# Weight parts in whole tiles, and tokens weighted before they are split, in a two-layer decoder kernel with experts

## The chip, the core and the metric

The kernel runs on one core of one Trainium2 chip. The metric is device time in microseconds (us), 1342.04 as the median of three runs (1341.5 to 1342.77) before the change.

## The reference, cut to what matters

256 tokens of width 1024 pass two layers; each adds a mixer, a cross attention and a feed-forward part to `x`. In the second layer the last part is a choice of 2 of 8 experts for each token:

```python
h = rmsnorm(x, norm_ffn_w[l])          # x * rsqrt(mean(x*x) + EPS) * w
logits = h @ router_w                  # 8 experts
top_v, top_i = top_k(logits, 2)        # gates: softmax of the two
for e in range(8):                     # width 2816
    y = y + gates[..., e:e+1] * ((silu(h @ w_gate[e]) * (h @ w_up[e])) @ w_down[e])
x = x + y
```

Everything is fp32. A product of two fp32 matrices is made of rounded parts: each operand is written as a high part (rounded) and a low part (the rest), and three products (low with high, high with low, high with high) are added.

## The kernel before

**Weights.** All weights come in tiles of 128x2048 fp32 (1 MB) in one fixed order (`weight_order`). SP loads them into staging tiles (`wst`, `wsp`), as many ahead as staging tiles are free (`stage`, `load` L173). Each tile is split: ACT copies it, rounded, into the high part `wh`, in two halves of 1024 columns; DVE subtracts, staged minus high, into the low part `wl`. In the layers `halve` (L185) does that, in 512 or 1024 columns; in the expert stage `high` (L236) and `low` (L247) do it, each for half a tile. The parts live in tiles of half a weight (`Halves` L89): five buffers each of `wh` and `wl` in the layers, seven and six in the expert stage (`HALVES` L37, L376).

**The expert stage** has its order written out by hand for PE, ACT and DVE (L1559). 264 weight tiles are used one after the other, each in one call of `slot` (L261). In the slot of tile t ACT rounds tile t+2, DVE subtracts tile t+1, and PE uses tile t. An expert is 11 chunks of three tiles: two of gate and up weights, one of down weights. Four experts are *long* (up to 128 tokens, three products a part, 12 matmuls of 512 columns a tile), four are *short* (up to 64 tokens; high and low part side by side in one operand, 8 matmuls a tile). Long and short chunks alternate after six long ones, and the last are short; the down tile of a chunk is used one chunk of its kind later.

Small steps are *posted* to a later slot and a place in it: before the first high half on ACT (`act`), between the two halves on ACT or DVE (`act mid`, `dve mid`), or in or behind PE's products (`pe mid`, `pe`). They are: the silu, the multiplication and the split of the hidden values (`chain`, L1373 and L1411), turned by PE in between (tile `et`); the marks that list an expert's tokens as one-hot columns (`mark` L1506, tile `oh`); the gather of an expert's tokens; and, when an expert is left (`leave` L1437), the transposes of its marks (`eo`), the split of its result (`yh`, `yl`), the scatter (`ez`) and the addition to `x`.

**The gather** (L1224) makes an expert's tokens out of `x` and the one-hot columns: `x` is split into `hmh` and `hml` (`halves` L1210, ACT then DVE), for each of 8 slices of the width PE adds four products into PSUM, so that the two parts come out summed; ACT multiplies by the norm's weight, rounded (`highs` L1244), DVE multiplies again and subtracts (`lows` L1248). The first gather runs before the expert stage, behind routing, among the steps of `columns` (the norm's factor `ncol`); the others are posted, one slice a slot. Routing itself (`route` L1103) follows the last addition to `x` in the cross attention.

`slot` and `low`, which the change reorders, in the words of the code:

```python
        self.places("act")
        self.high(t + 2, 0)
        self.low(t + 1, 0)
        self.places("dve mid", "act mid")
        self.high(t + 2, 1)
        self.low(t + 1, 1)
        w = self.ready.pop(key)
        products[0](*w)
        self.places("pe mid")
        products[1](*w)
        self.places("pe")
```

Of the kernel before, what the change touches and what calls it, by code (L numbers as in the profile page):

```python
# [7 lines left out]
F32 = mybir.dt.float32  # L8
# [28 lines left out]
HALVES = (5, {"wh": 2, "wl": 1})  # L37
# [49 lines left out]


class Halves:  # L89


    def __init__(self, *tiles):
        self.tiles = tiles

    def __getitem__(self, at):
        p, s = at
        h = s.start // 1024
        return self.tiles[h][p, s.start - h * 1024:s.stop - h * 1024]


class Trunk:
# [80 lines left out]
    def halves(self, name):  # L182
        return Halves(*[next(self.pools[name]).tile([P, 1024], F32R, name=name) for _ in range(2)])

    def halve(self, slot, st):  # L185

        nc, tc = self.nc, self.tc
        wh, wl = self.halves("wh"), self.halves("wl")
# [47 lines left out]
    def high(self, i, q):  # L236

        if i >= len(self.order) or i < self.nsplit:
            return
        if q == 0:  # L240
            self.stage()
            self.parts[i] = *self.loaded.pop(0), self.halves("wh"), self.halves("wl")
        _, st, wh, _ = self.parts[i]
        s = slice(q * 1024, (q + 1) * 1024)
        self.nc.scalar.activation(wh[:, s], st[:, s], AF.Copy)  # L245

    def low(self, i, q):  # L247
        if i not in self.parts:
            return
        slot, st, wh, wl = self.parts[i]  # L250
        s = slice(q * 1024, (q + 1) * 1024)
        with self.tc.issue_after(self.hold.ins) if self.hold else nullcontext():
            self.nc.vector.tensor_tensor(wl[:, s], st[:, s], wh[:, s].bitcast(F32), op=ALU.subtract)  # L253
        if q == 1:
            self.hold = None
            self.ready[self.order[i][0]] = wh, wl
            del self.parts[i]
            self.free.append(slot)
            self.stage()

    def slot(self, key, *products):  # L261
        t = self.nused
        assert self.order[t][0] == key, (self.order[t][0], key)
        self.now += 1
        if t + 1 < len(self.order) and t + 1 >= self.nsplit and t + 1 not in self.parts:
            self.high(t + 1, 0)
# [12 lines left out]
        self.nused += 1  # L279

    def rest(self):

        self.now += 1
        self.places("act", "dve mid", "act mid", "pe mid", "pe")


    def build(self):
# [6 lines left out]
        self.wp = pool("wp", HALVES[0])  # L294
        self.pools = {n: repeat(self.wp) for n in ("wh", "wl")}
# [77 lines left out]
        with tc.tile_pool(name="emid", bufs=1) as self.md, tc.tile_pool(name="ewkb", bufs=2) as self.wb, \  # L373
                tc.tile_pool(name="wst2", bufs=STAGES[1]) as wst2, ExitStack() as more:
            self.free += [slot(wst2)] * STAGES[1]
            for n, k in HALVES[1].items():  # L376
                p = more.enter_context(tc.tile_pool(name=f"{n}2", bufs=k))
                self.pools[n] = cycle([p] * k + [self.wp] * HALVES[0])
# [630 lines left out]
    def xattn(self, l):  # L1009
# [191 lines left out]
    def moe(self, j, l):  # L1201
# [22 lines left out]
        def gather(lists, xg):  # L1224
# [12 lines left out]
            def products(k):  # L1237
                ps[k] = self.psum(name="xg")
                for s in range(2):
                    for i in range(NT):  # L1240
                        nc.tensor.matmul(ps[k][:, lo:lo + w], hm[1 - s][:, i, k * P:(k + 1) * P], ohs[:, i, lo:lo + w],
                                         start=s == 0 and i == 0, stop=s == 1 and i == NT - 1)

            def highs(k):  # L1244
                for t, c in zip(xg, at):
                    self.split_hi(t[:, k, 0], ps[k][:, c], norm.w[:, k:k + 1])

            def lows(k):  # L1248
                for t, c in zip(xg, at):
                    self.gathered = self.split_lo(t[:, k, 0], t[:, k, 1], ps[k][:, c], norm.w[:, k:k + 1])  # L1250
# [11 lines left out]
            def steps():  # L1262
                for k in range(KD):
                    products(k)
                    highs(k)
                    lows(k)
# [4 lines left out]
            def spread(n):  # L1271

                for k in range(KD):
                    self.post(n + k, "pe", lambda k=k: products(k))
                    self.post(n + k + 1, "act mid", lambda k=k: highs(k))
                    self.post(n + k + 2, "dve mid", lambda k=k: lows(k))
                self.post(n + KD, "pe", scales)
                self.post(n + KD + 1, "dve mid", keep_scales)
# [88 lines left out]
        def long(x, xr):  # L1367
# [5 lines left out]
            def chain(pg):  # L1373
# [10 lines left out]
                self.post(1, "dve mid", lambda: nc.vector.scalar_tensor_tensor(  # L1384
# [3 lines left out]
                self.post(2, "dve mid", lambda: self.split_lo(*h, pt))  # L1388
# [8 lines left out]
        def short(x, xr):  # L1397
# [13 lines left out]
            def chain(pg):  # L1411
# [13 lines left out]
                self.post(2, "dve mid", lambda: nc.vector.tensor_tensor(s, s, pt[:, 2:4, :], op=ALU.mult))  # L1425
                self.post(2, "act mid", lambda: self.split_hi(hs[:, :, 0, :], s))
                self.post(3, "dve mid", lambda: self.split_lo(hs[:, :, 0, :], hs[:, :, 1, :], s))
# [9 lines left out]
        def leave(ps, oh, gate):  # L1437
# [18 lines left out]
            for n in range(2):  # L1456
                self.post(1 + n, "act", lambda n=n: self.split_hi(y[n][0], ps[n]))
                self.post(1 + n, "dve mid", lambda n=n: self.split_lo(*y[n], ps[n]))
            self.post(1, "dve mid", lambda: nc.vector.tensor_copy(oT, po[:, 0:T]))
            for n in range(2):  # L1460
                for i in range(NT):
                    pz = self.psum(name="ez")
                    self.post(2 + 2 * n + i, "pe", lambda pz=pz, i=i, n=n: scatter(pz, i, n))
                    self.post(3 + 2 * n + i, "dve mid", lambda pz=pz, i=i, n=n: add(pz, i, n))
# [51 lines left out]
        def prepare():  # L1516
# [3 lines left out]
            halves(1, 1)  # L1520
            return at, steps()

        def spread(n):
            marks, _, rest = lists_of(n)
            for i, m in enumerate(marks):
                self.post(1 + i, "dve mid", m)
# [84 lines left out]
    def final_weights(self):  # L1611
# [11 lines left out]
        for k in range(8):  # L1623
            b = k // 4
            self.post(1 + k, "dve mid", lambda k=k: diagonal(k))
# [26 lines left out]
def pack(inputs):  # L1652
# [23 lines left out]
    def chan(m):  # L1676

        L = m.shape[0]
        if m.ndim == 2:
# [17 lines left out]
                              [bias, chan(np.stack([g["norm_final_w"]] * DEPTH))], axis=2)  # L1697
    a["xq"] = fm(g["xattn_w_q"])
# [24 lines left out]
```

## Time and profile before

| what | value |
|---|---|
| median of three runs | 1342.04 us (1341.5 to 1342.77) |
| the profiled execution, its own time | 1343.5 us |
| its span, first to last instruction | 1341.6 us |
| mean granted TensorE clock | 0.990 |
| ACT, busy | 937.6 us (70%) |
| POOL, busy | 7.5 us (1%) |
| DMA, over the span | 368.06 MB, mean 274 GB/s |

The profile is that of one execution. Engines: PE multiplies, PEld loads PE's stationary operand, DVE is the vector engine, ACT the scalar engine, POOL GpSimd, SP the queue that issues loads. A row of a timeline gives the start in us from the span's start, the length, the engine, the line, the operation, output and inputs, shapes and, in brackets, how long the engine sat idle before it and what ended that. `x4` behind a row means four like it, one after the other. Matmuls are pipelined: the distance of two starts is what one costs.

### The profile page before, as it was taken

To read this page: it belongs to the slowest core of one execution; us is meant where nothing else is said; L and a number is where in the kernel's file an instruction comes from. 1 tells how busy PE (TensorE), PEld (TensorE's weight loads), DVE (VectorE), ACT (ScalarE), POOL (GpSimd) and SP (SyncE) were. 2 spreads that over 40 slices of the span, in tenths; PEclk is the share of its full clock that TensorE was granted. 3 is DMA by queue.
4 is the path that set the end of the run, shared out by engine and by line. 5 is a ranking of instruction groups with operands and counts; after the bars stand their busy time and mean duration, and the time that the engine had idled before them with its cause. 6 is when DMAs were issued, how large, how long until landed. Compare 5 with 4: busy or idle time off the path is not lost.

```text
span 1341.6 us, 20691 instructions
## 1 busy us (share of the span) xinstructions
PE 1293.9 (96%) x7301; PEld 1087.7 (81%) x7301; DVE 1162.9 (87%) x2057; ACT 937.6 (70%) x1502; POOL 7.5 (1%) x30
## 2 busy tenths in 40 slices
PE   9999999999999999989999999999999999999995
PEld 8978989999999878778877787777877778777773
DVE  8998877666677988579999999999999999999997
ACT  7565575444465556558788788887888887887884
POOL 0000000000000000000000000000000000000000
PEclk9999999999999999979999999999999999999998
DMA  8423625555544424549999999999999999999990
GB/s 326 158 96 118 228 95 194 187 187 189 187 165 151 164 95 160 194 149 338 343 405 386 338 371 413 379 402 338 355 412 384 394 380 337 404 407 371 392 351 34
DMA packets 67567, 368.06 MB, mean 274 GB/s; under 512 B 5744, under 2 KB 6000, under 8 KB 38016
## 3 DMA queue, kind: packets, MB, share of 16 engines
q1 hardware_dynamic: 67136, 365.59, 72.1%
q8 instruction: 59, 0.97, 0.3%
q0 software_dynamic: 320, 1.08, 0.2%
q14 instruction: 52, 0.43, 0.1%
HBM read 365.60 MB, written 1.05 MB: 273 GB/s over the span
## 4 chain that ended last, share of the span: by engine, by line
PE 68%; DVE 20%; issue 7%; ACT 5%; DMA 0%; DVEq 0%; SPq 0%; ACTq 0%
DVE wl L253 12%; PE fm L437 5%; PE fm L439 5%; PE fm L438 5%; PE eg L437 5%; PE eg L439 5%; PE eg L438 5%; PE ed L1433 4%; PE ed L437 2%; PE ed L438 2%; PE ed L439 2%; PE et L1420 2%; PE pr L437 2%; PE pr L438 2%; PE pr L439 2%
## 5 line engine op out<-in xcount | busy, mean ns | idle before, releaser
L253 DVE TENSOR_TENSOR wl<-wst,wh 128x1024 fp32r<-128x1024 f32 x294 | 348.9, 1222 | 0.0
L245 ACT ACTIVATE wh<-wst 128x1024 fp32r<-128x1024 f32 x294 | 295.6, 1053 | 0.0
L195 DVE TENSOR_TENSOR wl<-wst,wh 128x512 fp32r<-128x512 f32 x328 | 214.8, 688 | 87.9 <-ACT wh L191 87.7
L253 DVE TENSOR_TENSOR wl<-wsp,wh 128x1024 fp32r<-128x1024 f32 x232 | 276.1, 1222 | 1.5 <-PE eg L438 1.5
L191 ACT ACTIVATE wh<-wst 128x1024 fp32r<-128x1024 f32 x164 | 171.3, 1062 | 143.7 <-PE fm L439 88.5
L245 ACT ACTIVATE wh<-wsp 128x1024 fp32r<-128x1024 f32 x232 | 234.4, 1054 | 0.3 <-PE eg L439 0.3
L437 PE MATMUL fm<-hTh,wl 128*128 128x256 f32 x736 | 207.6, 282 | 1.0 <-DVE wl L195 1.0
L438 PE MATMUL fm<-hTl,wh 128*128 128x256 f32 x736 | 206.2, 280 | 0.0
L439 PE MATMUL fm<-hTh,wh 128*128 128x256 f32 x736 | 205.9, 280 | 0.0
L1409 PE MATMUL eg<-wl,xs 128*128 128x512 f32 x352 | 143.9, 409 | 5.9 <-DVE wl L253 5.9
L437 PE MATMUL eg<-wh,xg 128*128 128x512 f32 x352 | 141.2, 401 | 0.0
L437 PEld LDWEIGHTS fm<-hTh,wl 128*128 128x128 f32 x736 | 138.3, 188 | 1.9 <-DVE wl L195 1.2
L438 PE MATMUL eg<-wl,xg 128*128 128x512 f32 x352 | 139.8, 397 | 0.0
L439 PE MATMUL eg<-wh,xg 128*128 128x512 f32 x352 | 139.8, 397 | 0.0
L438 PEld LDWEIGHTS fm<-hTl,wh 128*128 128x128 f32 x736 | 138.2, 188 | 0.8 <-issue 0.2
L439 PEld LDWEIGHTS fm<-hTh,wh 128*128 128x128 f32 x736 | 138.7, 188 | 0.0
L1409 PE MATMUL eg<-wh,xs 128*128 128x512 f32 x352 | 138.6, 394 | 0.0
L1433 PE MATMUL ed<-wl,ehh 128*128 128x512 f32 x176 | 78.1, 444 | 13.5 <-DVE wl L253 12.2
L1409 PEld LDWEIGHTS eg<-wl,xs 128*128 128x128 f32 x352 | 66.3, 188 | 23.4 <-DVE wl L253 10.7
L439 PEld LDWEIGHTS eg<-wh,xg 128*128 128x128 f32 x352 | 66.8, 190 | 15.7
L437 PEld LDWEIGHTS eg<-wh,xg 128*128 128x128 f32 x352 | 67.0, 190 | 14.8
L438 PEld LDWEIGHTS eg<-wl,xg 128*128 128x128 f32 x352 | 66.9, 190 | 14.8
(339 smaller groups left out, 2257.0 us busy)
## 6 DMA issues: line engine op xcount, KB each, us to landing
wst<-in_moe_gu_dram SPq DMA_DIRECT2D x115, 1024.0 KB, 7.0
wsp<-in_moe_gu_dram SPq DMA_DIRECT2D x61, 1024.0 KB, 6.9
wsp<-in_moe_w_down_dram SPq DMA_DIRECT2D x55, 1024.0 KB, 7.2
wst<-in_moe_w_down_dram SPq DMA_DIRECT2D x33, 1024.0 KB, 7.3
wst<-in_ffn_gu_dram SPq DMA_DIRECT2D x22, 1024.0 KB, 4.9
wst<-in_w_in_fm_dram SPq DMA_DIRECT2D x16, 1024.0 KB, 4.9
wst<-in_ffn_w_down_dram SPq DMA_DIRECT2D x11, 1024.0 KB, 4.9
wst<-in_w_in_tm_dram SPq DMA_DIRECT2D x8, 1024.0 KB, 5.0
```

Source lines behind the costliest of these rows:

```text
L191: self.halved = nc.scalar.activation(wh[:, s], st[:, s], AF.Copy)
L195: nc.vector.tensor_tensor(wl[:, s], st[:, s], wh[:, s].bitcast(F32), op=ALU.subtract)
L245: self.nc.scalar.activation(wh[:, s], st[:, s], AF.Copy)
L253: self.nc.vector.tensor_tensor(wl[:, s], st[:, s], wh[:, s].bitcast(F32), op=ALU.subtract)
L437: nc.tensor.matmul(out, ll, rh, start=start, stop=False)
L438: nc.tensor.matmul(out, lh, rl, start=False, stop=False)
L439: nc.tensor.matmul(out, lh, rh, start=False, stop=stop)
L1409: nc.tensor.matmul(pg, both[:, c], w[:, fs], start=c == 0 and w is wl, stop=c == KD - 1 and w is wh)
L1420: nc.tensor.matmul(pt[:, b, :], g[:, b * P:(b + 1) * P], comb, start=True, stop=True)
L1433: nc.tensor.matmul(ps[n], h[:, k], w[:, fs], start=start and w is wl, stop=stop and w is wh)
```

## The change

Weight parts become whole tiles of 128x2048, three buffers each of `wh` and `wl` for the whole kernel. ACT still rounds in two halves; in the expert stage DVE subtracts a whole tile at once, and the steps of `dve mid` come behind it, in a place now called `dve`. `halve` in the layers keeps its pieces. In the short chunk the rounding of the hidden values goes from `act mid` of one slot to `act` of the next.

Tokens are multiplied by the norm's weight before they are split, by POOL (`xw`, four products of 128x512), with the weight as a row on all partitions, loaded by a broadcast from a new input `wrow` into the tile that later holds the output. That tile is also a staging tile; it is withheld until the last product is issued. The gather keeps the two parts apart, side by side in PSUM, and ACT copies both with one instruction; DVE's `lows` are gone.

```diff
-HALVES = (5, {"wh": 2, "wl": 1})
+SPLITS = {"wh": 3, "wl": 3}
...
+    def parts_of(self):
+        return [self.wp.tile([P, 2048], F32R, name=n, bufs=SPLITS[n]) for n in ("wh", "wl")]
...
-    def low(self, i, q):
+    def low(self, i):
         if i not in self.parts:
             return
-        slot, st, wh, wl = self.parts[i]
-        s = slice(q * 1024, (q + 1) * 1024)
+        slot, st, wh, wl = self.parts.pop(i)
         with self.tc.issue_after(self.hold.ins) if self.hold else nullcontext():
-            self.nc.vector.tensor_tensor(wl[:, s], st[:, s], wh[:, s].bitcast(F32), op=ALU.subtract)
-        if q == 1:
-            self.hold = None
-            self.ready[self.order[i][0]] = wh, wl
-            del self.parts[i]
-            self.free.append(slot)
-            self.stage()
+            self.nc.vector.tensor_tensor(wl, st, wh.bitcast(F32), op=ALU.subtract)
+        self.hold = None
+        self.ready[self.order[i][0]] = wh, wl
+        self.free.append(slot)
+        self.stage()
...
         self.places("act")
         self.high(t + 2, 0)
-        self.low(t + 1, 0)
-        self.places("dve mid", "act mid")
+        self.low(t + 1)
+        self.places("dve", "act mid")
         self.high(t + 2, 1)
-        self.low(t + 1, 1)
...
             self.o = self.spare()().rearrange("p (i d) -> p i d", i=NT)
+            self.later = self.free.pop()
+            self.wrow = self.o[:, 0, :]
+            nc.gpsimd.dma_start(self.wrow, a["wrow"].to_broadcast([P, D]))
             self.spare()
...
         def halves(i, n):
             s = slice(n * 512, (n + 1) * 512)
-            self.split(hm[0][:, i, s], hm[1][:, i, s], self.x[:, i, s])
+            xw = wb.tile([P, 512], F32, name="xw", tag="yh" if n else "yl")
+            nc.gpsimd.tensor_tensor(xw, self.x[:, i, s], self.wrow[:, s], op=ALU.mult)
+            self.split(hm[0][:, i, s], hm[1][:, i, s], xw)
...
             def products(k):
-                ps[k] = self.psum(name="xg")
+                ps[k] = self.psum((P, 2, 2 * P), "xg")
                 for s in range(2):
                     for i in range(NT):
-                        nc.tensor.matmul(ps[k][:, lo:lo + w], hm[1 - s][:, i, k * P:(k + 1) * P], ohs[:, i, lo:lo + w],
-                                         start=s == 0 and i == 0, stop=s == 1 and i == NT - 1)
-
-            def highs(k):
-                for t, c in zip(xg, at):
-                    self.split_hi(t[:, k, 0], ps[k][:, c], norm.w[:, k:k + 1])
-
-            def lows(k):
-                for t, c in zip(xg, at):
-                    self.gathered = self.split_lo(t[:, k, 0], t[:, k, 1], ps[k][:, c], norm.w[:, k:k + 1])
+                        nc.tensor.matmul(ps[k][:, s, lo:lo + w], hm[s][:, i, k * P:(k + 1) * P], ohs[:, i, lo:lo + w],
+                                         start=i == 0, stop=i == NT - 1)
+
+            def keep(k):
+                for t, c in zip(xg, at):
+                    self.gathered = nc.scalar.activation(t[:, k], ps[k][:, :, c], AF.Copy)
...
-                    self.post(n + k + 1, "act mid", lambda k=k: highs(k))
-                    self.post(n + k + 2, "dve mid", lambda k=k: lows(k))
+                    self.post(n + k + 1, "act mid", lambda k=k: keep(k))
...
-                self.post(2, "act mid", lambda: self.split_hi(hs[:, :, 0, :], s))
-                self.post(3, "dve mid", lambda: self.split_lo(hs[:, :, 0, :], hs[:, :, 1, :], s))
+                self.post(3, "act", lambda: self.split_hi(hs[:, :, 0, :], s))
+                self.post(3, "dve", lambda: self.split_lo(hs[:, :, 0, :], hs[:, :, 1, :], s))
...
             halves(1, 1)
+            self.free.append(self.later)
             return at, steps()
```

## Rows read from the trace of the kernel before

**Rows 1.** The page, engines: busy us, share of the span, instructions.
```profile
PE 1293.9 (96%) x7301; PEld 1087.7 (81%) x7301; DVE 1162.9 (87%) x2057; ACT 937.6 (70%) x1502; POOL 7.5 (1%) x30
```

**Rows 2.** The page, costliest groups: count, busy us, mean ns of one, idle before.
```profile
L253 DVE TENSOR_TENSOR wl<-wst,wh 128x1024 fp32r<-128x1024 f32 x294 | 348.9, 1222 | 0.0
...
L195 DVE TENSOR_TENSOR wl<-wst,wh 128x512 fp32r<-128x512 f32 x328 | 214.8, 688 | 87.9 <-ACT wh L191 87.7
...
L437 PE MATMUL fm<-hTh,wl 128*128 128x256 f32 x736 | 207.6, 282 | 1.0 <-DVE wl L195 1.0
```

**Rows 3.** Timeline of PE: first such pair's hole, one pair, last hole.
```profile
674.35 0.50 PE L1433 MATMUL ed<-wl,ehh 128*128 128x512 f32 x1 [0.15 <-DVE wl L253]
...
700.72 0.48 PE L1409 MATMUL eg<-wl,xs 128*128 128x512 f32 x1
...
704.47 0.40 PE L1433 MATMUL ed<-wl,ehh 128*128 128x512 f32 x1
...
705.30 0.50 PE L1433 MATMUL ed<-wl,ehh 128*128 128x512 f32 x1 [0.20 <-DVE wl L253]
...
705.87 1.00 PE L1420 MATMUL et<-comb,eg 128*128 128x64 f32 x8
...
716.22 0.48 PE L1409 MATMUL eg<-wl,xs 128*128 128x512 f32 x1
...
1203.21 0.50 PE L1433 MATMUL ed<-wl,ehh 128*128 128x512 f32 x1 [0.19 <-DVE wl L253]
```

**Rows 4.** Timeline of ACT in that pair.
```profile
698.38 2.00 ACT L245 ACTIVATE wh<-wst 128x1024 fp32r<-128x1024 f32 x2
701.00 0.38 ACT L447 ACTIVATE ehh<-et 128x256 fp32r<-128x256 f32 x1 [0.62 <-PE et L1381]
701.28 3.90 ACT L245 ACTIVATE wh<-wsp 128x1024 fp32r<-128x1024 f32 x4
```

**Rows 5.** Timeline of DVE in that pair.
```profile
701.41 0.43 DVE L451 TENSOR_TENSOR ehl<-et,ehh 128x256 fp32r<-128x256 f32 x1
...
702.89 4.63 DVE L253 TENSOR_TENSOR wl<-wsp,wh 128x1024 fp32r<-128x1024 f32 x4
```

**Rows 6.** Timeline of DVE where a long expert is left.
```profile
732.15 0.29 DVE L1509 TENSOR_SCALAR oh<-twice,sorted 128x128 fp32r<-128x128 bf16 x1 [2.24 <-PE eo L1445]
...
734.62 0.42 DVE L451 TENSOR_TENSOR ehl<-et,ehh 128x256 fp32r<-128x256 f32 x1
...
736.08 2.35 DVE L253 TENSOR_TENSOR wl<-wst,wh 128x1024 fp32r<-128x1024 f32 x2
```

**Rows 7.** Timeline of PE there.
```profile
737.35 0.50 PE L1409 MATMUL eg<-wl,xs 128*128 128x512 f32 x1 [1.39 <-DVE wl L253]
...
740.99 1.00 PE L1420 MATMUL et<-comb,eg 128*128 128x64 f32 x8
```

**Rows 8.** Timeline of PE where a short expert is left.
```profile
851.01 0.48 PE L1409 MATMUL eg<-wl,xs 128*128 128x512 f32 x1
...
857.79 1.00 PE L1420 MATMUL et<-comb,eg 128*128 128x64 f32 x8
```

**Rows 9.** Timeline of PE ahead of the first chunk.
```profile
591.57 1.01 PE L1256 MATMUL xr<-ncol,oh 128*128 128x1 f32 x4 [3.54 <-DVE ncol L467]
```

**Rows 10.** Timeline of DVE there.
```profile
591.43 0.61 DVE L453 SCALAR_TENSOR_TENSOR xg<-xg,prm 128x128 fp32r<-128x128 f32 x2
```

**Rows 11.** Timeline of POOL, its products.
```profile
3.02 0.38 POOL L913 TENSOR_SCALAR half<-prm 128x62 f32<-128x62 f32 x1 [1.33 <-DMA prm<-in_prm_dram]
3.38 0.20 POOL L914 TENSOR_SCALAR half<-prm 128x2 f32<-128x2 f32 x1
...
135.19 1.88 POOL L913 TENSOR_SCALAR half<-prm 128x62 f32<-128x62 f32 x1 [50.53 <-DVE catl L453]
```

**Rows 12.** Timeline of DVE beside the last of them.
```profile
134.93 1.89 DVE L195 TENSOR_TENSOR wl<-wst,wh 128x512 fp32r<-128x512 f32 x3
```

**Rows 13.** Waits from 690 to 1330 us: us in total, times, longest.
```profile
PEld ed L1433 <- DVE wl L253: 30.6, 41, 1.4
```

More of the change, by code (lines that the diff above doesn't have):

```diff
@@ L1 @@
 from contextlib import ExitStack, nullcontext
-from itertools import chain, cycle, islice, repeat
+from itertools import chain, islice
 import concourse.bass as bass
@@ L86 @@
     pass
[L89 to L98, printed above, removed]
 class Trunk:
@@ L180, in load @@
         return slot, st
-    def halves(self, name):
-        return Halves(*[next(self.pools[name]).tile([P, 1024], F32R, name=name) for _ in range(2)])
+    def parts_of(self):
+        return [self.wp.tile([P, 2048], F32R, name=n, bufs=SPLITS[n]) for n in ("wh", "wl")]
     def halve(self, slot, st):
         nc, tc = self.nc, self.tc
-        wh, wl = self.halves("wh"), self.halves("wl")
+        wh, wl = self.parts_of()
         for q in range(2):
@@ L241, in high @@
             self.stage()
-            self.parts[i] = *self.loaded.pop(0), self.halves("wh"), self.halves("wl")
+            self.parts[i] = *self.loaded.pop(0), *self.parts_of()
         _, st, wh, _ = self.parts[i]
@@ L283, in rest @@
         self.now += 1
-        self.places("act", "dve mid", "act mid", "pe mid", "pe")
+        self.places("act", "dve", "act mid", "pe mid", "pe")
     def build(self):
@@ L293, in build @@
         self.free = [slot(self.wst)] * STAGES[0]
-        self.wp = pool("wp", HALVES[0])
-        self.pools = {n: repeat(self.wp) for n in ("wh", "wl")}
+        self.wp = pool("wp", 1)
         self.ps = pool("ps", 8, space=PSUM)
@@ L373, in build @@
         with tc.tile_pool(name="emid", bufs=1) as self.md, tc.tile_pool(name="ewkb", bufs=2) as self.wb, \
-                tc.tile_pool(name="wst2", bufs=STAGES[1]) as wst2, ExitStack() as more:
+                tc.tile_pool(name="wst2", bufs=STAGES[1]) as wst2:
             self.free += [slot(wst2)] * STAGES[1]
-            for n, k in HALVES[1].items():
-                p = more.enter_context(tc.tile_pool(name=f"{n}2", bufs=k))
-                self.pools[n] = cycle([p] * k + [self.wp] * HALVES[0])
             self.xg = [self.big("xg", shape=(P, 2 * KD * P)) for _ in range(2)]
@@ L1264, in steps @@
                     products(k)
-                    highs(k)
-                    lows(k)
+                    keep(k)
                     yield
@@ L1387, in chain @@
                 self.post(2, "act", lambda: self.split_hi(h[0], pt))
-                self.post(2, "dve mid", lambda: self.split_lo(*h, pt))
+                self.post(2, "dve", lambda: self.split_lo(*h, pt))
                 return h
@@ L1457, in leave @@
                 self.post(1 + n, "act", lambda n=n: self.split_hi(y[n][0], ps[n]))
-                self.post(1 + n, "dve mid", lambda n=n: self.split_lo(*y[n], ps[n]))
-            self.post(1, "dve mid", lambda: nc.vector.tensor_copy(oT, po[:, 0:T]))
+                self.post(1 + n, "dve", lambda n=n: self.split_lo(*y[n], ps[n]))
+            self.post(1, "dve", lambda: nc.vector.tensor_copy(oT, po[:, 0:T]))
             for n in range(2):
@@ L1463, in leave @@
                     self.post(2 + 2 * n + i, "pe", lambda pz=pz, i=i, n=n: scatter(pz, i, n))
-                    self.post(3 + 2 * n + i, "dve mid", lambda pz=pz, i=i, n=n: add(pz, i, n))
+                    self.post(3 + 2 * n + i, "dve", lambda pz=pz, i=i, n=n: add(pz, i, n))
         class Expert:
@@ L1525, in spread @@
             for i, m in enumerate(marks):
-                self.post(1 + i, "dve mid", m)
+                self.post(1 + i, "dve", m)
             rest(1 + len(marks))
@@ L1697, in pack @@
                               [bias, chan(np.stack([g["norm_final_w"]] * DEPTH))], axis=2)
+    a["wrow"] = g["norm_ffn_w"][1:2]
     a["xq"] = fm(g["xattn_w_q"])
```

8 lines of the change are left out of this document (4 added, 4 removed).

## The prediction

> **What bounds the kernel now.** I read the page first: in the expert stage (from about 590 us on) PE, DVE and ACT are all busy nearly all the time, and over the span PE has 96% and DVE 87% [rows 1]. A share that high names two candidates and doesn't decide between them, so next come the costliest groups: what changes is the split of a weight tile, one DVE subtraction (`wl`) for each half of 1024 columns, at 1222 ns; the same operation on 512 columns takes 688 ns [rows 2]. In the layers before, PE's costliest products waited 1.0 us in all for `wl` [rows 2]; so the stage that counts is the expert stage, and its timeline is read engine by engine.
>
> There the work repeats in pairs: a long chunk (three weight tiles: gate/up, gate/up, down, 12 matmuls each) and a short one (three tiles, 8 matmuls each). One pair runs from 700.72 to 716.22 [rows 3], 15.5 us. The matmuls follow each other every 0.23 us with one hole: the short down tile begins at 704.47, its third matmul only at 705.30, because the second half of its `wl` wasn't there; the block `et` behind it starts at 705.87 [rows 3]. Four matmuls should take 0.92 us, they took 1.40: 0.48 lost. 25 pairs look like this one, from the hole ending at 674.35 to that ending at 1203.21 [rows 3]. So PE bounds the pair, but for one handoff.
>
> Follow that handoff back. PE ends the long down tile and turns the long chunk's hidden values; at 701.00 ACT, which had waited 0.62 us for that, rounds them (`ehh`), and only then, at 701.28, come the high halves of the short down tile, every 0.95 us (four in 3.90, two in 2.00; one lasts 1.05) [rows 4]. DVE subtracts `ehl` at 701.41, finishes the tile before, and at 702.89 begins four halves, one every 1.14 us; the second ends at 705.25 [rows 5], and PE goes on 0.05 later. The hole is the end of a chain PE, ACT, DVE, PE that starts anew in each pair; a share of busy time doesn't show it.
>
> **The weight split in whole tiles.** One subtraction of 2048 columns instead of two: 1222 ns + 2 x (1222 - 688) = 2.29 us (1024 more columns at the slope of the two forms) [rows 2]. It must wait for both high halves, and PE may not start on the tile before all of it is there. In the pair above, with X = 700.72: the high halves end at 701.28 + 0.95 + 1.05 = 703.28 [rows 4]; 0.03 later (701.38 to 701.41) [rows 4, 5] DVE starts; it is free, for the tile before has its high halves at 698.38 + 2.00 = 700.38 [rows 4], is subtracted by 702.70, and `ehl` (0.34 to the next operation) follows. So `wl` is whole at 703.31 + 2.29 = 705.60, PE restarts at 705.65 and needs 4 x 0.23 + 0.10 (the refill seen from 705.30 to 705.87, two matmuls in 0.57) = 1.02: `et` at 706.67 instead of 705.87. That is **+0.80 us a pair, and 25 pairs make +20.0**. Nothing later in the pair gives it back: the other five tiles of a pair had no hole, and their work on PE is the same. DVE is relieved (per tile 2 x 1.14 - 2.21 = 0.07), but DVE isn't what the hole waits for then; the tile is handed over in one piece, after two serial ACT halves.
>
> The ring of parts says the same from another side. `wh` had seven half tiles in this stage, now three whole ones, so the high half for tile t+2 waits until PE has done all of tile t-1. For the short down tile that is the long down tile, whose end ACT waits for anyway; no further cost there. Behind ACT's wait stand only later high halves and the copies of gathered tokens; behind DVE's new wait for both halves stand the posted steps of that tile, and for the short down tile there are none. The short chunk's own rounding moves one tile later on ACT; its down tile comes a pair later still.
>
> **Places of the chain steps.** The posted steps on DVE (multiply, `ehl`, marks, evacuation, adds) now come after the whole subtraction instead of between its halves. That costs nothing in the pair above and helps in the pairs where an expert is left. After a long one a mark waits 2.24 us for the transposes `eo` and holds up, in DVE's order, the second half that PE needs; the sequel is PE waiting until 737.35 and `et` only at 740.99 [rows 6, 7]. With the change the first short tile is complete before that mark. Then: mark at 732.15 + 0.20, whole tile to 734.65, the four small steps 1.46 (734.62 to 736.08) [rows 6], whole tile 736.1 to 738.4, `et` at 738.45 + 1.02 = 739.5: -1.5 each, three of them, **-4.5**. After a short one `et` comes 6.78 after the pair's X [rows 8]; the chain of the pair gives 4.93 + 1.02 = 5.95: -0.8 each, three of them, **-2.5**.
>
> **The other pairs.** The first short chunk has no down tile before it, so the chain strikes the long tile behind it: estimate +1.3, from a place without a hole today. Three pairs with a gather in them have one or two copies more between the two high halves, but longer PE slots: estimate +0.5 each. Three late pairs, where the long down tile comes last: +0.4 each. The closing chunks are short only; there the ring closes on itself over three tiles, about +1 in all. Together **+5.0**; all from the chain above with the other order of tiles.
>
> **The gather.** DVE loses 64 small subtractions (8 slices for each of 8 experts), ACT gets wider copies (two parts, one instruction), PE keeps its four matmuls a slice. Inside the chunks this is covered by PE. Before the first chunk it isn't: PE waits 3.54 us there for `ncol` [rows 9], and DVE runs eight of those subtractions among the steps that make it and the first weight splits, two in 0.61 [rows 10]. Without them: 8 x 0.3 = -2.4.
>
> **POOL's product.** Four products of 128x512 are new, in front of the first split. No row shows one. POOL's 62-column product took 0.38 us once and 1.88 the other time; its two-column one 0.20 [rows 11]. The slow one ran beside three DVE subtractions with two SBUF inputs, 134.93 to 136.82 [rows 12], and ended when they had ended. That gives 0.2 + 510 x 3 ns = 1.7 us alone, and 510 x 28 ns = 14 us at worst. [...] I take 1.7, since in front of the gather DVE has no run of weight splits to stand behind, as it had there. The 16 us of routing hide four times 1.7, save that ACT or DVE may queue behind the first: +0 to +2, taken as 0, like the stretch itself, which ends on DVE and PE. The broadcast load of the weight row goes to POOL's own queue, ahead of the products; the staging tile withheld for it leaves eight of nine on SP's: nothing, or one transfer's delay if they run dry.
>
> **The layers before.** Three whole tiles instead of five halves free a tile's second half earlier and its first no later. PE waited 1.0 us there: 0, at most +-2 by a changed order.
>
> **The sum** is 20.0 - 4.5 - 2.5 + 5.0 - 2.4 = +15.6. The profiled execution has 1343.5 us (span 1341.6), 1.5 above the median 1342.0; it becomes 1359.1, the median 1357.6, called 1358.
>
> **Rivals.** *DVE's relief decides.* In favour: DVE's share, and that PE's hole names `wl`; PE waited 30.6 us in all for it in the short down tiles, as its weight loads show [rows 13]. If the handoff in one piece cost nothing, DVE would gain 0.07 for each of 264 tiles, of which 0.42 a pair fills its hole of 0.48: 25 x 0.42 = 10.5, with the 7.0 of the leaving experts and the 2.4 of the gather: -20, 1322 us. It decides if `et` comes less than 5.15 (705.87 - 700.72) behind X. Against it: the chain leaves DVE waiting, not working. [...] *POOL holds the routing.* With 14 us each the fourth product would end at 568 + 57 = 625, where the gather starts at 584 now: +41, about 1400. It decides from some 4 us each. *The change does less than it says:* if the whole subtraction were still handed over by halves, all pairs stay as they are and only the leaving experts and the gather count: -9.4, 1333.
>
> **Chances.** Forecast 0.86, of which 0.03 in a flank below 1345; relief 0.08, POOL 0.03, less than it says 0.03. A measurement of this kernel tells 0.2%, 2.7 us, from no change. Faster 0.11, same 0.03, slower 0.86. The low end takes 0.6 a pair (without the refill and the two short latencies, 0.18 together), -9 at the leaving experts, -3.5 at the gather (all that PE waits there) and -2 in the layers: +5.5, 1348. The high end takes 0.95 (the short gate tile is ready at 702.70, PE wants it at 702.56, and this may add up), no gain at the gather, POOL's 2 and the layers' 2: +26, 1368. The other cases fall outside, with 0.14.
>
> **What would show it.** Right: in the steady pairs a period of 16.3, whole subtractions of 2.29, `wl` ready 4.9 behind X, DVE idle before them with ACT's `wh` as releaser, and PE waiting 1.2 at the start of the short down tile; about -2 before the first chunk. Wrong: pairs of 15.1, or DVE without idle time, or PE waiting on hm's parts before the gather.

## The result, and the profile after

| kernel | median | runs | ratio to before |
|---|---|---|---|
| before, same chip | 1342.4 us (1341.5 to 1343.88) | 4 | 1 |
| after | 1363.84 us (1362.34 to 1366.57) | 4 | 1.0161 [1.0142, 1.018] |

Slower by 21.4 us; forecast were 15.6, and 1358 (1348 to 1368). The spans of the two profiled executions, 1362.5 and 1341.6, differ by 20.9.

The page of after, engines, then its costliest groups; beside [rows 1, 2]:

```profile
PE 1298.4 (95%) x7301; PEld 1087.1 (80%) x7301; DVE 1136.0 (83%) x1730; ACT 938.4 (69%) x1502; POOL 12.2 (1%) x35
...
L242 DVE TENSOR_TENSOR wl<-wst,wh 128x2048 fp32r<-128x2048 f32 x148 | 337.2, 2290 | 30.6 <-ACT wh L234 29.8
...
L242 DVE TENSOR_TENSOR wl<-wsp,wh 128x2048 fp32r<-128x2048 f32 x115 | 262.7, 2290 | 39.7 <-ACT wh L234 38.9
...
L1415 PE MATMUL ed<-wl,ehh 128*128 128x512 f32 x176 | 77.4, 440 | 29.7 <-DVE wl L242 27.4
```

DVE works 27 us less than before, and the kernel is 21 us slower. The groups say why in their last column: DVE now stands idle for 70.3 us ahead of the whole subtractions (68.7 of them with ACT's high half as the releaser), and PE idles for 29.7 us ahead of the short down tile (27.4 with `wl` as the releaser). Before, DVE's halves of `wst` had no idle time at all [rows 2].

One steady pair of after, PE's timeline (X is 704.43):

```profile
704.43 0.48 PE L1391 MATMUL eg<-wl,xs 128*128 128x512 f32 x1
...
708.15 0.40 PE L1391 MATMUL eg<-wh,xs 128*128 128x512 f32 x1
709.37 0.50 PE L1415 MATMUL ed<-wl,ehh 128*128 128x512 f32 x1 [0.82 <-DVE wl L242]
...
710.40 1.00 PE L1402 MATMUL et<-comb,eg 128*128 128x64 f32 x8
...
720.75 0.48 PE L1391 MATMUL eg<-wl,xs 128*128 128x512 f32 x1
```

ACT and DVE in the same pair:

```profile
704.71 0.38 ACT L429 ACTIVATE ehh<-et 128x256 fp32r<-128x256 f32 x1 [0.65 <-PE et L1363]
704.99 2.00 ACT L234 ACTIVATE wh<-wsp 128x1024 fp32r<-128x1024 f32 x2
```

```profile
704.09 2.29 DVE L242 TENSOR_TENSOR wl<-wst,wh 128x2048 fp32r<-128x2048 f32 x1 [0.41 <-ACT wh L234]
706.30 0.42 DVE L433 TENSOR_TENSOR ehl<-et,ehh 128x256 fp32r<-128x256 f32 x1
707.02 2.29 DVE L242 TENSOR_TENSOR wl<-wsp,wh 128x2048 fp32r<-128x2048 f32 x1 [0.30 <-ACT wh L234]
```

The chain of [rows 3 to 5] has become longer. ACT ends its second high half at 706.99, DVE has been idle for 0.30 and starts at 707.02, `wl` is whole at 709.31 (X + 4.88; 4.88 were forecast), and PE, done with the gate tiles since 708.38, starts the down tile at X + 4.94. `et` follows at X + 5.97 (forecast 5.95; before 5.15 [rows 3]). The period is 16.32 (forecast 16.3). One sign came out smaller: from the end of the gate tiles PE waits 0.99, where 1.2 was forecast, because the gate tiles themselves ended 0.2 later behind X than in the pair of [rows 3].

To book the 20.9 us I subtracted, between the two traces, the start of ACT's silu `es` of each long chunk (44 in either):

| term | forecast | measured |
|---|---|---|
| 25 steady pairs | +20.0 | +21.6 (0.83 to 0.95 each) |
| three leaves of a long expert | -4.5 | -4.5 (-1.53, -1.58, -1.41) |
| three leaves of a short expert | -2.5 | -2.6 (-0.69, -0.76, -1.13) |
| other pairs | +5.0 | +5.5 (first short chunk 1.1, gathers 0.42, 0.42 and 0.54, two late pairs 0.47 and 0.49, the rest to the end 2.0) |
| up to and with the first chunk's matmuls | -2.4 | +0.9 |
| sum | +15.6 | +20.9 |

One term has the wrong sign, the one up to the first chunk. It is made of three pieces: the gap between the first gather and the first chunk shrank by 0.17 us, the stretch from the first of the four last additions to `x` to that gather is 17.25 where it was 16.61, and some 0.4 lies elsewhere, most of it ahead of that, where profiles of the same code differ by more. Its rows of after, beside [rows 9, 10], PE first and then DVE:

```profile
588.64 0.39 PE L1229 MATMUL xg<-oh,hml 128*128 128x128 f32 x2
592.42 0.99 PE L1240 MATMUL xr<-ncol,oh 128*128 128x1 f32 x4 [3.39 <-DVE num L1162]
593.27 0.77 PE L419 MATMUL eg<-wh,xg 128*128 128x512 f32 x1
```

```profile
586.51 2.28 DVE L242 TENSOR_TENSOR wl<-wst,wh 128x2048 fp32r<-128x2048 f32 x1
588.71 0.15 DVE L449 SCALAR_TENSOR_TENSOR ncol<-rs_t,ncol 128x2 f32<-128x2 f32 x1
...
588.98 2.29 DVE L242 TENSOR_TENSOR wl<-wst,wh 128x2048 fp32r<-128x2048 f32 x1
...
591.38 0.16 DVE L449 SCALAR_TENSOR_TENSOR ncol<-rs_t,ncol 128x2 f32<-128x2 f32 x1
...
592.12 0.16 DVE L449 SCALAR_TENSOR_TENSOR ncol<-rs_t,ncol 128x2 f32<-128x2 f32 x1
```

The small subtractions are gone, and PE waits 3.39 us for `ncol` all the same (3.54 before): two whole subtractions stand among the small steps that make it, and hold each step behind them for 2.2 us. Before, four halves stood there (1.14 us each to the next instruction):

```profile
584.57 1.22 DVE L253 TENSOR_TENSOR wl<-wst,wh 128x1024 fp32r<-128x1024 f32 x1
...
586.50 1.22 DVE L253 TENSOR_TENSOR wl<-wst,wh 128x1024 fp32r<-128x1024 f32 x1
...
588.36 1.22 DVE L253 TENSOR_TENSOR wl<-wst,wh 128x1024 fp32r<-128x1024 f32 x1
...
590.23 1.22 DVE L253 TENSOR_TENSOR wl<-wst,wh 128x1024 fp32r<-128x1024 f32 x1
...
591.36 0.16 DVE L467 SCALAR_TENSOR_TENSOR ncol<-rs_t,ncol 128x2 f32<-128x2 f32 x1
```

So the weights take as long between these steps as they did. Six of the eight small subtractions stood there too (0.26 us each, 1.6 together); the two of [rows 10] come behind the last `ncol`. In their place nine small steps of routing have moved in, 1.0 us together. (In after, the row of `xr` names `num`, the last DVE instruction ahead of it; `ncol` itself had been there 0.14 us before.)

POOL's products cost 1.3 each, not 1.7; but beside the second of them DVE's first `hml` took 1.60 us, where the three that follow take 0.68 to 0.69, as all did before:

```profile
570.69 1.28 POOL L1199 TENSOR_TENSOR xw<-x,wsp 128x512 f32<-128x512 f32 x1 [0.47 <-DVE x L618]
```

```profile
570.91 1.60 DVE L433 TENSOR_TENSOR hml<-xw,hmh 128x512 fp32r<-128x512 f32 x1 [0.31 <-ACT hmh L429]
```

### The profile page after: what moved, and what is told of

Read it like the earlier page. It is cut to its first block, busy times and chain, and to the rows that moved or that the text cites. A ratio compares the mean times of both kernels' runs of the same rounds, so it can differ in the third digit from the quotient of the medians.

```text
span 1362.5 us, 20101 instructions
## 1 busy us (share of the span) xinstructions
PE 1298.4 (95%) x7301; PEld 1087.1 (80%) x7301; DVE 1136.0 (83%) x1730; ACT 938.4 (69%) x1502; POOL 12.2 (1%) x35
## 4 chain that ended last, share of the span: by engine, by line
PE 74%; DVE 13%; ACT 8%; issue 3%; DMA 1%; SPq 0%; POOL 0%; ACTq 0%; DVEq 0%; POOLq 0%
DVE wl L242 7%; PE ed L1415 7%; PE eg L419 6%; PE eg L420 6%; PE eg L421 6%; ACT wh L234 6%; PE fm L419 5%; PE fm L421 5%; PE fm L420 5%; PE ed L419 3%; PE ed L420 3%; PE ed L421 3%; PE et L1402 3%; PE pr L419 2%; PE pr L421 2%
## 5 line engine op out<-in xcount | busy, mean ns | idle before, releaser
L242 DVE TENSOR_TENSOR wl<-wst,wh 128x2048 fp32r<-128x2048 f32 x148 | 337.2, 2290 | 30.6 <-ACT wh L234 29.8
L242 DVE TENSOR_TENSOR wl<-wsp,wh 128x2048 fp32r<-128x2048 f32 x115 | 262.7, 2290 | 39.7 <-ACT wh L234 38.9
L1415 PE MATMUL ed<-wl,ehh 128*128 128x512 f32 x176 | 77.4, 440 | 29.7 <-DVE wl L242 27.4
L420 PEld LDWEIGHTS eg<-wl,xg 128*128 128x128 f32 x352 | 66.8, 190 | 16.3 <-DVE wl L242 1.2
```

The costliest lines, as they stand in the source:

```text
L242: self.nc.vector.tensor_tensor(wl, st, wh.bitcast(F32), op=ALU.subtract)
L420: nc.tensor.matmul(out, lh, rl, start=False, stop=False)
L1415: nc.tensor.matmul(ps[n], h[:, k], w[:, fs], start=start and w is wl, stop=stop and w is wh)
```

## The experiments

Each ran beside the kernel before on one chip, whose median there was 1342.73 (E1 to E4), 1342.85 (E5 to E8) or 1343.53 (E9 to E11); ratios are to that. "Gap" is the time from the first matmul of the first gather (`xg`) to the first of the first chunk (`eg`); "period" the time between the copies `eg` of two steady short chunks.

| kernel | median us | ratio to before | period | gap |
|---|---|---|---|---|
| before (profile shown above) | 1342.4 | 1 | 15.47 | 8.18 |
| after | 1363.84 | 1.0161 [1.0142, 1.018] | 16.33 | 8.01 |
| E1 two subtractions | 1332.55 | 0.9929 [0.9909, 0.9949] | 15.44 | 6.60 |
| E2 tokens alone | 1340.66 | 0.9987 [0.9977, 0.9997] | 15.47 | 5.90 |
| E3 parts alone | 1361.82 | 1.0152 [1.013, 1.0173] | 16.33 | 7.98 |
| E4 steps behind | 1335.12 | 0.9948 [0.9932, 0.9964] | 15.41 | 8.59 |
| E5 copy first | 1332.26 | 0.9915 [0.9892, 0.9937] | 15.1 | 8.12 |
| E6 held | 1356.98 | 1.0097 [1.0076, 1.0118] | 16.33 | 4.02 |
| E7 product on DVE | 1362.11 (one run) | | 16.33 | 8.49 |
| E8 late rounding | 1347.91 | 1.0036 [1.0023, 1.0049] | 15.84 | 8.12 |
| E9 all, half tiles | 1324.06 | 0.986 [0.9845, 0.9876] | 15.1 | 4.02 |
| E10 all, whole tiles | 1323.81 | 0.9853 [0.9836, 0.987] | 15.1 | 4.02 |
| E11 as E9, copy late | 1329.78 | 0.9906 [0.989, 0.9922] | 15.41 | 4.02 |

The span before routing differs between these profiles by some us even where the code there is the same (E4 reached routing 1.3 us earlier than before; the granted clock from 550 to 562 us was 1.00 in E4 and 0.86 in before). So below I read periods and gaps, and medians for the whole; each profile is one execution.

**E1, the whole subtraction cut in two.**

```diff
-            self.nc.vector.tensor_tensor(wl, st, wh.bitcast(F32), op=ALU.subtract)
+            for q in range(2):
+                s = slice(q * 1024, (q + 1) * 1024)
+                self.nc.vector.tensor_tensor(wl[:, s], st[:, s], wh[:, s].bitcast(F32), op=ALU.subtract)
```

> The changed kernel with its one whole subtraction in the expert stage cut into two halves of 1024 columns, issued one behind the other; tiles, ring of three and the places of the steps stay. Theory (handoff in one piece): the first half may start when ACT's first high half is done, so in a steady pair the parts of the short down tile are ready about 3.1 and 4.3 us behind X (the start of the short gate tile), PE wants them at 3.95 and 4.4, the hole of 1.0 us goes, the period falls from 16.33 to about 15.1 and the time to about 1331 (1326 to 1337). Rival (the ring of three whole tiles, or the later rounding of the short chunk, makes the hole): the period stays at 16.3 and the time at 1362 to 1366.

Measured: 1332.55, 31 us less than after, with the same tiles, the same ring and the same places. The down tile starts at X + 3.76 without a hole (X is 697.50). But the period is 15.44, not 15.1. PE, DVE and ACT of that pair, and a row of the waits from 690 to 1320 us:

```profile
701.26 0.39 PE L1417 MATMUL ed<-wl,ehh 128*128 128x512 f32 x1
701.49 0.39 PE L1417 MATMUL ed<-wh,ehh 128*128 128x512 f32 x1
701.72 0.40 PE L1417 MATMUL ed<-wl,ehh 128*128 128x512 f32 x1
701.96 0.39 PE L1417 MATMUL ed<-wh,ehh 128*128 128x512 f32 x1
702.49 1.10 PE L1404 MATMUL et<-comb,eg 128*128 128x64 f32 x8
```

```profile
699.14 2.36 DVE L244 TENSOR_TENSOR wl<-wsp,wh 128x1024 fp32r<-128x1024 f32 x2 [0.22 <-ACT wh L234]
```

```profile
699.95 2.00 ACT L234 ACTIVATE wh<-wst 128x1024 fp32r<-128x1024 f32 x2
701.85 0.58 ACT L1406 ACTIVATE eg<-eg 128x512 f32<-128x512 f32 x1
```

```profile
PEld et L1404 <- ACT eg L1406: 15.4, 27, 0.7
```

`et` should follow at 702.19, 0.23 behind the fourth matmul. It comes at 702.49, because its input, ACT's copy `eg`, ended at 702.43: PE had finished the gate tiles at 701.26, but the copy stood in ACT's queue behind four high halves. The handoff made the hole of after; with it gone, the next wait shows. That the time came out right with a period 0.3 too long has other causes: I had counted the 25 pairs alone. From the first short chunk's copy `eg` to the last E1 needs 650.9 where after needs 678.0, and only 22 of these 27 us are steady pairs (25 x 0.88); the closing chunks give another 1.6 (from the 38th copy to the last 50.9 in E1, 52.5 in after, 51.1 before), and the gap is 1.4 shorter.

**E2 and E3, the change in its two parts.** E2 is the kernel before with the product on POOL, the two parts kept apart in PSUM and ACT's one copy; E3 is after without these. E2 against before, its core:

```diff
+            nc.gpsimd.tensor_tensor(xw, self.x[:, i, s], self.wrow[:, s], op=ALU.mult)
+            self.split(hm[0][:, i, s], hm[1][:, i, s], xw)
...
-                    highs(k)
-                    lows(k)
+                    keep(k)
```

> The kernel before, with the tokens' part of the change alone (product on POOL before the split, parts side by side in PSUM, one copy by ACT, no small subtractions on DVE). Theory: only the stretch ahead of the first chunk changes, where POOL's product slows DVE's split and freed places on DVE are taken by other steps: 0 to +1 us, 1342.4 to 1343.5, the long subtraction hml (0,0) again near 1.6 us. Rival (my sum on record): 2.4 us less, 1340. Rival (DVE's relief inside the chunks with a gather reaches PE): 5 us less or more, 1337.

> The changed kernel without the tokens' part: whole tiles, one subtraction, steps behind it, tokens split and gathered as before. Theory: all but the 0.8 us ahead of the first chunk comes from here: 20 us more than before, 1361 to 1364, period of the steady pairs 16.3. Rival (the copies of two parts by ACT between its high halves are what delays the handoff): under 1355.

Measured: E2 is 2.1 us faster than before, so the theory (0 to +1) fell, and the number is that of the prediction's sum (-2.4): the gap shrinks by 2.28, from 8.18 to 5.90, although `hml` took 1.38. E3 keeps the gap (7.98) and has nearly the whole loss (+19.1), so ACT's wider copies are not what delays the handoff. The gain of E2 does not add to E3: after, which has both, has a gap of 8.01. Inside the chunks E2 changes nothing: its steady periods are those of before, so with this order of steps DVE's 64 fewer subtractions are worth nothing there. In E2's profile the first chunk was 2.4 us shorter as well; that execution was the fastest of its ten (1338.08), the median's 2.1 us fit the gap alone, and whether the others had the shorter chunk isn't known. PE in E2, ahead of the first chunk, then DVE's halves among the steps of `ncol`, three now:

```profile
589.06 0.58 PE L1258 MATMUL xr<-ncol,oh 128*128 128x1 f32 x4 [1.40 <-DVE ncol L467]
```

```profile
584.37 1.22 DVE L253 TENSOR_TENSOR wl<-wst,wh 128x1024 fp32r<-128x1024 f32 x1
...
585.77 1.22 DVE L253 TENSOR_TENSOR wl<-wst,wh 128x1024 fp32r<-128x1024 f32 x1
...
587.17 1.22 DVE L253 TENSOR_TENSOR wl<-wst,wh 128x1024 fp32r<-128x1024 f32 x1
```

One half fewer is 1.14 of the 2.28 us. The small subtractions that left, 1.6, less the steps of routing that moved in here, 0.9, give 0.7, and the four matmuls of `xr` took 0.44 less.

**E4 and E5, half tiles with the change's order of steps.** E4 is the kernel before with DVE's posted steps behind both halves, and the short chunk's rounding one tile later. E5 also puts the copy `eg` ahead of a high half (`owe` is true in a short chunk's second gate tile). E4 against before, then E5 against E4:

```diff
         self.low(t + 1, 0)
-        self.places("dve mid", "act mid")
+        self.places("act mid")
         self.high(t + 2, 1)
         self.low(t + 1, 1)
+        self.places("dve mid")
...
-                self.post(2, "act mid", lambda: self.split_hi(hs[:, :, 0, :], s))
+                self.post(3, "act", lambda: self.split_hi(hs[:, :, 0, :], s))
```

```diff
         self.places("act")
+        if self.owed:
+            self.high(t + 1, 1)
+        self.owed = owe
...
-        self.high(t + 2, 1)
+        if not owe:
+            self.high(t + 2, 1)
```

> The kernel before, half tiles and all, with one thing of the change alone: DVE's posted steps come behind both halves of a tile, and the short chunk rounds its hidden values one tile later. Theory: the tile before the short down tile is split before DVE takes ehl, so the second half of the down tile is ready about 3.9 us behind X where PE wants it at 4.2: the hole of 0.48 us in 25 pairs goes (period 15.0), the leaving experts give 1.5 and 0.8 each as in the changed kernel: 19 us less, 1323 (1320 to 1330). Rival (DVE as a whole is too busy, so the hole only moves): period 15.5, and only the leaves' 7 us: 1335.

> Half tiles, DVE's steps behind both halves as in e4_steps_behind, and one more step: behind a short chunk's second gate tile ACT copies eg before the second high half of the tile after next, no longer behind it. Theory (in e4 the handoff of the down tile left the path, and et then waits 0.3 us for the copy of eg, which stands in ACT's queue behind four high halves): the copy starts when PE ends the gate tile, et follows the four matmuls of the down tile at once, the period falls from 15.42 to 15.1, 25 pairs give 8 us, 1327 (1323 to 1331). Rival (the late high half makes a new hole at the long gate tile behind it): period 15.4 or more, 1334 to 1337.

Measured: E4 is 7.6 us faster than before, the rival's number but not its reason. By the silus of the long chunks the gain lies where experts are left: the six pairs in which one is left are 8.4 us shorter together, the three with a gather behind a long one 1.9 longer. The hole in the down tile did go, and yet the period is 15.41; what holds it is not DVE. ACT and PE of E4, then of E5:

```profile
699.44 3.90 ACT L245 ACTIVATE wh<-wsp 128x1024 fp32r<-128x1024 f32 x4
703.25 0.58 ACT L1423 ACTIVATE eg<-eg 128x512 f32<-128x512 f32 x1
```

```profile
703.33 0.40 PE L1434 MATMUL ed<-wh,ehh 128*128 128x512 f32 x1
703.88 1.10 PE L1421 MATMUL et<-comb,eg 128*128 128x64 f32 x8 [0.15 <-ACT eg L1423]
```

```profile
700.87 2.95 ACT L245 ACTIVATE wh<-wsp 128x1024 fp32r<-128x1024 f32 x3
704.26 0.60 ACT L1429 ACTIVATE eg<-eg 128x512 f32<-128x512 f32 x1 [0.44 <-PE eg L1416]
```

```profile
704.79 0.39 PE L1440 MATMUL ed<-wh,ehh 128*128 128x512 f32 x1
705.02 1.00 PE L1427 MATMUL et<-comb,eg 128*128 128x64 f32 x8
```

In E4 the four high halves end at 703.34 and the copy at 703.83, 0.05 ahead of `et`. In E5 ACT waits for PE, the copy ends at 704.86, and `et` follows the four matmuls after 0.23. The pairs fall to 15.1, as expected. The time, 1332.26, lies above its range and below the rival's. From one long chunk's silu to the next, the pair in which a short expert is left grew from 16.9 to 17.6 us in E5, three times; the pair in which a long one is left takes 19.15 in both.

**E6, the first split and the rest of routing held behind `ncol`.**

```diff
-            nc.vector.scalar_tensor_tensor(y, t, 1.5, y, op0=ALU.add, op1=ALU.mult)
+            self.rooted = nc.vector.scalar_tensor_tensor(y, t, 1.5, y, op0=ALU.add, op1=ALU.mult)
...
-            self.hold = at
+            self.hold = self.rooted
...
-        with tc.issue_after(self.gathered.ins):
+        with tc.issue_after(self.rooted.ins):
```

> The changed kernel with the first subtraction of the expert stage, and the rest of routing on DVE, held until the last step that makes ncol. Theory (two whole subtractions between the steps of ncol take what the removed small subtractions gave): xr and the first chunk no longer wait, first gather to first chunk about 5 us in place of 8.0, 3 us less than the changed kernel, 1361 or less on the same footing as 1363.8. Rival (the gather on PE and ACT, or the first weight tile, sets it): 7 us or more, less than 1 us gained.

Measured: the gap is 4.02, half of what it was, and the time 6.9 us below after. PE waits for nothing any more:

```profile
587.39 0.39 PE L1229 MATMUL xg<-oh,hml 128*128 128x128 f32 x2
587.62 0.55 PE L1240 MATMUL xr<-ncol,oh 128*128 128x1 f32 x4
588.03 0.48 PE L419 MATMUL eg<-wh,xg 128*128 128x512 f32 x1
```

Two things were moved at once; by their size the two whole subtractions (4.4 us between the steps in after) count for more than the nine steps of routing (1.0), but they were not tried apart. The gap is 4.0 of the gain; another 2.3 lies in the first chunk, whose matmuls, up to its silu, take 5.88 us in place of 8.21. The first 6 us of that chunk, in after and in E6: the stretch and its length, busy times of PE, PEld, DVE, ACT and POOL, the granted clock, then DMA:

```profile
593.00:599.00 6.00, 6.00 (x17) 4.80 (x18) 2.05 (x13) 2.26 (x5) 0.00 (x0) 0.55 0.03 13
```

```profile
588.00:594.00 6.00, 6.00 (x28) 4.87 (x28) 5.93 (x24) 4.54 (x10) 0.00 (x0) 1.00 0.48 175
```

Behind a wait of 3.39 us PE ran at a mean granted clock of 0.55 (in windows of half a microsecond it is 0.50 from 592.0 to 598.0 and 1.00 from 598.5 on), with 17 matmuls where E6, at 1.00, has 28.

**E7, the product on DVE.**

```diff
-            nc.gpsimd.tensor_tensor(xw, self.x[:, i, s], self.wrow[:, s], op=ALU.mult)
+            nc.vector.tensor_tensor(xw, self.x[:, i, s], self.wrow[:, s], op=ALU.mult)
```

> The changed kernel with the four products of tokens and weights on DVE in place of POOL. Theory (POOL's product beside it is what stretches DVE's subtraction hml (0,0) from 0.69 to 1.60 us): hml takes 0.69 each time, the products 0.7 each; the time stays within 2 us of 1363.8. Rival (reading xw, or a wait inside the instruction, stretches it): 1.6 again.

Measured, DVE's row of the same subtraction:

```profile
570.40 0.68 DVE L433 TENSOR_TENSOR hml<-xw,hmh 128x512 fp32r<-128x512 f32 x1
```

POOL's product was what stretched it: without it all four `hml` of E7 take 0.68 to 0.69, where the first of after took 1.60. In after the stretched `hml` ends at 572.51, 0.54 behind POOL's product (571.97); in E1 0.55 behind it (569.20 + 1.62 against 568.98 + 1.29), in E2 0.55. These ends fit a DVE that stood until POOL was all but done and then took its usual 0.68 (in after from 571.83 on). At half its speed beside POOL it would have ended some 0.15 behind it in after; that is an estimate from these times: of 1.06 us beside POOL half counts as done, and 0.15 of the 0.68 is left. What holds DVE isn't shown, nor what it costs the kernel: the one run of E7, at 1362.11, lies beside after's lowest, and its gap is longer (8.49).

**E8, the long chunk's rounding behind the high halves.**

```diff
         self.high(t + 2, 1)
+        self.places("act end")
...
-                self.post(2, "act", lambda: self.split_hi(h[0], pt))
-                self.post(2, "dve", lambda: self.split_lo(*h, pt))
+                self.post(2, "act end", lambda: self.split_hi(h[0], pt))
+                self.post(3, "dve", lambda: self.split_lo(*h, pt))
```

> The changed kernel with the long chunk's rounding ehh behind the slot's two high halves on ACT, and ehl one tile later on DVE. Theory (ACT's wait for the turned hidden values and the ring of three wh are met one behind the other: without the first, the high half may start as soon as PE has left the long down tile): the high halves of the short down tile start 0.05 behind X in place of 0.56, its wl is ready 4.4 behind X in place of 4.9, period 15.8, 12 us less than the changed kernel, about 1351. Rival (the ring frees the tile later than X, or DVE isn't free): period 16.3, no change; and if the late ehl is missed by the next long down tile, longer.

Measured: period 15.84, 15.9 us less than after; the 25 pairs give the 12 that were expected, and the rest was not followed up. ACT in a pair with X = 703.17:

```profile
703.23 2.01 ACT L234 ACTIVATE wh<-wsp 128x1024 fp32r<-128x1024 f32 x2 [0.42 <-PE ed L422]
```

The high half starts 0.06 behind X, and now the releaser is PE's last long down matmul, the ring. So the ring of three was a second wait behind ACT's wait for `et`, hidden by it. With whole tiles handed over whole, ACT's start is on the path: starting 0.50 us earlier gave 0.49 a pair.

**E9 to E11, what is worth keeping.** E9 is E5 with the tokens' part and the hold of E6; E10 is E1 with E5's copy and the hold; E11 is E9 without the copy first. The edits are those above.

> Half tiles as before; DVE's steps behind both halves, the copy of eg ahead of the second high half (e5_copy_first), the tokens' part of the change, and the first subtraction of the expert stage and the rest of routing held behind ncol (e6_held). If the gains add: 1332.3 of e5_copy_first, less 4 us between first gather and first chunk (4.0 in place of 8.1), 2 us of PE's clock behind it, and 2 us at the leaving experts: about 1324 (1321 to 1328). If the gather's gain overlaps with what PE waits anyway, or the steps of the tokens come in each other's way: 1329 or more.

> The changed kernel's whole tiles in a ring of three, with two subtractions of half a tile (e1_two_subtractions), the copy of eg ahead of the second high half, and the hold behind ncol. If whole tiles are harmless once they are handed over by halves: within 3 us of e9_all_halves, about 1325 (1322 to 1330). Rival (with the copy first, the ring of three whole tiles becomes the limit): steady pairs of 15.4, 1330 or more.

> As e9_all_halves without the copy of eg ahead of the second high half: the same gains on top of e4_steps_behind: 1335.1 less 8, about 1327 (1324 to 1331). If the copy first is worth at the pairs what it cost at the leaves, equal to e9_all_halves within 1 us.

Measured: 1324.06, 1323.81 and 1329.78. E9 and E10 can't be told apart; both beat the kernel before by 1.4 to 1.5%. Whole tiles and a ring of three cost nothing that these runs can tell once the parts are handed over by halves. The copy first is worth 5.7 us (E11 to E9). E11 was some 3 us above its expected value, near the upper end of its range. With the steps behind both halves the tokens' part does reach PE inside the chunks: the three pairs with a gather behind a leaving long expert take 18.66, 18.69 and 18.16 in E11, and 19.42, 19.42 and 18.41 in E4.

## Why the prediction was right, and where it was wrong

**The handoff** was the cause, at nearly the price forecast. The chain ehh, two high halves, whole subtraction, PE came out link by link: `wl` at X + 4.88, `et` at X + 5.97. E1 is the proof: the same tiles with two subtractions lose none of the 0.86 a pair. The term was slightly mis-sized: 0.80 against 0.86, over 25 pairs 1.6 us.

**Its order of steps** does help at the leaves, -4.5 and -2.6 as worked out; E4, with that order and half tiles, has -5.4 and -3.0 there.

**The ring** costs nothing further in the pairs, as said, and E8 shows the wait that lay hidden behind ACT's. At the closing chunks I had put +1 down to the ring closing on itself. That was wrong: E1 has the same ring and loses nothing there, so this too is the handoff, and all that follows the last late pair measured 2.0.

**The failed step is the gather**: "Without them: 8 x 0.3 = -2.4". The step counted what leaves DVE's queue between the steps of `ncol`, and not what else stands there or moves in. In after the gap shrank by 0.17. Two of the eight small subtractions were not between the steps at all (those of [rows 10]), the other six were worth 1.6, routing's steps took 1.0 of it back, and the weights stand between the steps as before, two wholes for four halves. E2's 2.28 has the forecast's size by luck: 1.14 of it is that three halves stood there instead of four, and with whole tiles that gain did not come. I had priced each part of the change beside the old form of the other. In the prediction's own list, "about -2 before the first chunk" was measured as +0.9 with all that lies ahead of it. That is 3.3 of the 5.3 us by which the sum was short: 2.2 the gap, 0.6 the stretch from the additions to `x` to the first gather, the rest ahead of that and in the first chunk. Of the other 2.0, 1.6 are the pairs, and the rest the closing chunks.

**POOL** was taken as hidden, at 0. With half tiles that held: from the first of the four last additions to `x` to the first gather it takes 16.57 us in E2, 16.61 before. With whole tiles it is 16.19 without the tokens' part (E3), 17.25 in after and 17.34 with the product on DVE (E7): about 1 us, on either engine; why isn't known. The price came from one row at 3 ns an element and was 1.28 instead of 1.7. That DVE would be held up (1.60 us for 0.68), and not only POOL [rows 11, 12], wasn't in the prediction.

**The rival, DVE's relief**, fell with its own test: `et` at X + 5.97, not under 5.15. DVE's busy time did fall by 27 us, and a whole takes 2.29 where two halves in a row take 2.36 (E1): 0.07 us saved a tile. Saving time on an engine that waits bought nothing here. The other way round, E1 cut each subtraction in two again, spent the 0.07 us, handed the first half over sooner, and was 31 us faster than after.

What stays open: why the pairs in which a short expert is left got longer in E5 was not tried; nor was a fourth whole `wh`, so what the ring costs behind E8's step is not known.

## What to carry to other kernels

Before merging two instructions, ask who waits for the first half: the time saved (0.07 us a tile here, 2.36 against 2.29) is small beside the handoff delayed (0.86 a pair). Price the parts of a change beside each other, not each beside the old code, and ask what will move into a place that is freed: here each of two whole subtractions of 2.29 us held the small steps of `ncol` behind it for 2.2, and PE waited 3.39 us where 3.54 had been. And when a hole is closed, look for what ends next in the same place; here it was a copy behind four high halves.

## What was not expected of the hardware

DVE's 128x512 subtraction `hml` took 1.60, 1.62 and 1.38 us (after, E1, E2) beside a POOL product of 1.28 to 1.29 us, and 0.68 in every other row of E1 and E2, 0.68 or 0.69 in after; the long ones ended 0.54 to 0.55 after POOL did.

Behind PE's waits ahead of the first chunk the granted clock was lower, and the chunk took longer. The granted clock in that chunk's first 6 us was 0.56 in before (behind a wait of 3.54), 0.55 in after (3.39), 0.72 in E3 (3.17) and 0.75 in E1 (2.22); it doesn't follow the length of the wait (0.64 behind 3.94 in E4). In windows of half a microsecond it is 0.50 up to 597.5 in before and up to 598.0 in after, and 1.00 from 598.0 and 598.5 on. With a wait of 1.40 (E2) or none (E6, E9, E11) the clock of these 6 us was 1.00, and PE has 27 or 28 matmuls in them, where it has 17 in before and in after. The chunk's matmuls up to its silu took 8.26 us in before, 8.21 in after and 5.88 in E6. In E6 the medians show it: 6.9 us less than after, where the gap gives 4.0. In E2 they don't: its median gained 2.1 us, which the gap alone gives.
